# Feed forward of a two-layer hybrid block: 12 of 22 column pairs by seven block products instead of eight

## The chip, the cores and the metric

The kernel runs on one core of a Trainium2 chip. The metric is device time in microseconds (us). The engines are named as in the profile: PE is TensorE's matmul, PEld its weight load, DVE is VectorE, ACT is ScalarE, POOL is GpSimd, SP is SyncE, which here only issues DMAs.

## The reference, cut to what matters

Two layers run over a sequence of 528 positions (16 learned ones and 512 tokens). Each layer has four mixers, a merge of them, an output projection, and then the feed forward that is changed here:

```
D_MODEL, D_FF = 1024, 2816
x = x + merged @ w_out
h2 = rmsnorm(x, norm_ffn)
gt, up = jnp.split(h2 @ w_gu, 2, axis=-1)        # 1024 -> 2 x 2816
return x + (jax.nn.silu(gt) * up) @ w_down       # 2816 -> 1024
```

All numbers are 32-bit floats.

## The kernel before, in words

Activations are kept transposed: a tile has 128 features in its partitions and the positions in its columns. The normalised input `h2` is eight such tiles, `hh[0..7]`, with eight more, `hl[0..7]`, that hold what is left over, because every operand of TensorE is split into a high part (ACT casts it, `split`, L199, or `wload`, L190) and a low part (DVE subtracts, L200 or L192), and every product is made of three: high times high, high weight times low input, low weight times high input (`mmk`, L206).

The 2816 columns of the gate and of the up matrix are 22 blocks of 128. Pair j is block j of both: 1024 inputs to 128 gate columns and 128 up columns. Pair 0 is done by `head`, beside the end of the norm; the others by `mm`. A product of 1024 by 128 has eight k-steps of three matmuls. In layer 0 the 528 positions are two segments of 264 columns, so a pair has 2 x 8 x 3 x 2 = 96 matmuls of 264 columns; layer 1 needs 512 positions only, one segment, so a pair has 48 matmuls of 512 columns. Then ACT takes the tanh of the gate out of PSUM (L365), DVE makes silu(gate) times up (L366, L1584), and `split` makes `ah` and `al` of it, the operands of the down projection.

The pairs are done in three groups (8, 7 and 7 pairs, `FFG`); after each group the down projection adds that group's share to the residual (`residual`, L1545). Weights come in tiles of 128 by 512 (four k-steps): a DMA of SP into `wr` (3 buffers), the cast into `wh` and the subtraction into `wl` (5 buffers each).

PE's instructions stand in the order in which the program is written. The order of ACT, DVE, POOL and SP is set by a scheduler from the dependences, the buffers and its own estimates; `after(...)` holds what is issued inside it behind the instructions named. Generators (`start`, `pump`, `need`) lay side work between the matmuls. One of them is `s5_prep`, the tables of the state space mixer: those of layer 0 are made during the mixers of layer 0, those of layer 1 during the first pairs of the feed forward of layer 0.

PSUM is eight banks: `psm` gives two at a time (2 such buffers), `psx` one (4 buffers).

Of the kernel before, what the change touches and what calls it, by code (L numbers as in the profile page):

```python
# [9 lines left out]
F32 = mybir.dt.float32  # L10
F32R = mybir.dt.float32r
U32 = mybir.dt.uint32
AF = mybir.ActivationFunctionType
ALU = mybir.AluOpType
AX = mybir.AxisListType

P = 128
D = 1024
KD = D // P
SEQ = 512  # L20
META = 16
T = SEQ + META
DEPTH = 2
# [3 lines left out]
KF = FF // P  # L27
# [26 lines left out]
    _o += _w  # L54
NPK = _o
FFG = [(0, 8), (8, 7), (15, 7)]


def halves(segs):
    t0 = segs[0][0]  # L60
    n = (T - t0) // 2
    return [(t0, n), (t0 + n, n)]


class Kern:
# [36 lines left out]
    def after(self, *inss):  # L102

        ctx = ExitStack()
        for ins in inss:
            ctx.enter_context(self.tc.issue_after(ins))
        return ctx
# [1386 lines left out]
        return bh, bl  # L1494


    def layer(self, l, xdram, segs, after):
        nc, a = self.nc, self.a
        t0 = segs[0][0]
        st, gdn = self.gdn_proj(l)  # L1500
        self.share = False
        qk, rv = self.ret_proj(l)
        self.mg = []
        for j in range(KD):
            if j == 4:
                gs = self.head_gates(l, C_DG, segs)
                while "m" not in st["done"]:
                    self.pump()
            if j % 4 == 0:
                mg = self.f4(name="mg")  # L1510
            self.mg.append(mg[:, j % 4, :])
            self.gate(self.mg[j], l, 3, j, segs)
        parts = self.head_finish(gdn, st["v"], gs, self.par(l, "gdn"), segs)
        glap = self.gla_proj(l)
        gst, gla = next(glap)
        ret = self.start(self.ret_gen(l, qk, rv))
        pst = {"go": False}
        if l == 0:
            prep = self.start(self.s5_prep(0, pst))
        self.merge(l, 3, *parts, segs, "first")  # L1520
        next(glap)
        self.need(ret)
        gst["done"] += "v"
        pst["go"] = True
        self.merge(l, 1, *self.head_finish(ret, rv, self.head_gates(l, C_RG, segs), self.par(l, "rtn"), segs), segs, "mid")
        sy = self.s5_proj(l)
        if l == 0:
            self.need(prep)
        self.need(gla)
        zh, zl = self.f4(F32R, "zh"), self.f4(F32R, "zl")  # L1530
        s5 = self.s5_gens(l, sy, zh, zl, t0)
        self.merge(l, 0, *self.head_finish(gla, gst["v"], self.head_gates(l, C_HG, segs), self.par(l, "hgn"), segs), segs,
                   "mid")
        parts = self.s5_finish(l, s5, sy, zh, zl, segs)
        self.mh, self.ml = [], []
        self.merge(l, 2, *parts, segs, "last")
        xt = [self.f4(name="x") for _ in range(2)]
        xs = [xt[j // 4][:, j % 4, :] for j in range(KD)]
        self.norm_new(segs, xs, self.norm_h(self.par(l, "nffn")))

        def residual(srcs, kt, xh, xl, old, norm):

            tail = KD - 2 if norm else KD
            for j, ps in enumerate(self.mms(srcs[:tail], kt, xh, xl, segs)):
                nc.vector.scalar_tensor_tensor(out=self.sv(xs[j], segs), in0=ps, scalar=0.5,  # L1545
                                               in1=self.sv(old(j), segs), op0=ALU.mult, op1=ALU.add)
                if norm:
                    self.norm_sq(j, (t0, T - t0))
            if norm:
                olds = [old(j) for j in range(tail, KD)]  # L1550

                def evac(i, ps, h):
                    s0, n = halves(segs)[h]
                    c = slice(s0, s0 + n)
                    nc.vector.scalar_tensor_tensor(out=xs[tail + i][:, c], in0=ps, scalar=0.5, in1=olds[i][:, c],  # L1555
                                                   op0=ALU.mult, op1=ALU.add)
                    self.nrm["last"] = self.norm_sq(tail + i, (s0, n), own=l + 1 == DEPTH and kt < KD and i == h == 1)
                self.mm2h(srcs[tail:], kt, xh, xl, segs, self.tail_hooks(kt), evac)

        def xold(j):  # L1560
            xo = self.f(name="xo")
            nc.sync.dma_start(xo[:, t0:], xdram[j][:, t0:])
            return xo

        residual([a["w_out"][l, j] for j in range(KD)], KD, self.mh, self.ml, xold, True)

        prep = None
        for g0, gn in FFG:
            ah, al = [], []
            for j in range(gn):  # L1570
                if j % 4 == 0:
                    h4, l4 = self.f4(F32R, "ah"), self.f4(F32R, "al")
                srcs = [a["w_gu"][l, o + g0 + j] for o in (0, KF)]
                sg = segs
                if g0 + j == 0:
                    sg = halves(segs)
                    pg, pu = self.head(srcs, segs)
                else:
                    pg, pu = (self.mm(self.wload(s, KD), KD, self.hh, self.hl, segs) for s in srcs)
                if g0 + j == 2 and l + 1 < DEPTH:  # L1580
                    prep = self.start(self.s5_prep(l + 1, {"go": True}))
                s = self.f(name="s")
                self.silu2(s, pg, sg)
                nc.vector.tensor_tensor(out=self.sv(s, sg), in0=self.sv(s, sg), in1=pu, op=ALU.mult)  # L1584
                hv, lv = h4[:, j % 4, :], l4[:, j % 4, :]
                self.split(hv[:, t0:], lv[:, t0:], s[:, t0:])
                ah.append(hv)
                al.append(lv)
            last = g0 + gn == KF
            if last:  # L1590
                self.need(prep)
                self.norm_new(segs, xs, after(), then=KD if l + 1 < DEPTH else 0)
            residual([a["w_dn"][l, j, :, g0 * P:(g0 + gn) * P] for j in range(KD)], gn, ah, al, lambda j: xs[j], last)
        return xs
# [182 lines left out]
```

## Time and profile before

| | us |
|---|---|
| median of 3 runs | 2227.5 (2225.49 to 2228.37) |
| profiled execution | 2226.7 |
| its span | 2224.9 |
| PE busy | 2202.2 (99%) |
| DVE busy | 1269.9 (57%) |
| ACT busy | 893.7 (40%) |

The span is the time from the first to the last instruction in the trace; the profiled execution is 1.8 us longer and 0.8 us under the median. A matmul's own duration in the trace overlaps the next one's, so what a matmul costs is read from how many start in a stretch, not from its duration.

### The profile page before, as it was taken

How to read it: one execution, taken by the hardware profiler on the slowest of the kernel's cores; microseconds unless marked ns; L12 is line 12 of the kernel's file. 1: busy time of each engine (PE TensorE's matmuls, PEld its weight loads, DVE VectorE, ACT ScalarE, POOL GpSimd, SP SyncE). 2: the span in 40 equal slices, each digit the busy share in tenths (PEclk: the TensorE clock that was granted, in tenths of full speed). 3: DMA queues.
4: the chain of work that ended last, by engine and by line, in shares of the span. 5: the costliest groups of instructions: out<-in, count | busy, mean ns of one | idle time of the engine just before them, and what ended most of it. 6: DMA issues, size and time to landing. Idle time of an engine off the chain costs nothing. (4 is left out here: it accounts for less than half of the span.)

```text
span 2224.9 us, 41086 instructions
## 1 busy us (share of the span) xinstructions
PE 2202.2 (99%) x16300; PEld 2019.0 (91%) x16300; DVE 1269.9 (57%) x2505; ACT 893.7 (40%) x1920; POOL 189.5 (9%) x243
## 2 busy tenths in 40 slices
PE   9999999999999999999999999999999999999998
PEld 8999999999999999999999988787888888888887
DVE  7884566758444677533367844745385445434344
ACT  5653544433333433322346534644333334323232
POOL 2420021110000100000014121000000001000000
PEclk9999999999999999999999999999999999999999
DMA  4332222374233234332232332222643332332322
GB/s 129 104 105 66 86 77 77 111 228 141 89 91 119 96 110 124 124 87 94 88 119 83 106 95 83 75 72 72 202 122 90 95 123 91 90 100 91 98 93 83
DMA packets 144540, 229.73 MB, mean 103 GB/s; under 512 B 30044, under 2 KB 46884, under 8 KB 143836
## 3 DMA queue, kind: packets, MB, share of 16 engines
q1 hardware_dynamic: 136572, 208.98, 30.5%
q0 software_dynamic: 4032, 11.70, 1.6%
q10 hardware_dynamic: 3744, 6.42, 0.8%
q8 instruction: 128, 2.10, 0.4%
q14 instruction: 64, 0.52, 0.1%
HBM read 207.40 MB, written 19.65 MB: 102 GB/s over the span
## 5 line engine op out<-in xcount | busy, mean ns | idle before, releaser
L190 ACT CAST wh<-wr 128x512 fp32r<-128x512 f32 (+1 forms) x680 | 416.7, 614 | 1019.7 <-PE pm L206 841.7
L206 PE MATMUL pm<-hh,wh 128*128 128x264 f32 (+1 forms) x3120 | 799.6, 315 | 3.0 <-ACT hh L199 1.6
L206 PE MATMUL pm<-hl,wh 128*128 128x264 f32 (+1 forms) x3120 | 787.4, 312 | 5.6 <-POOL hl L200 2.9
L206 PE MATMUL pm<-hh,wl 128*128 128x264 f32 (+1 forms) x3120 | 783.2, 310 | 0.0
L192 DVE TENSOR_TENSOR wl<-wr,wh 128x512 fp32r<-128x512 f32 (+1 forms) x664 | 460.1, 695 | 537.3 <-ACT wh L190 528.3
L206 PEld LDWEIGHTS pm<-hh,wh 128*128 128x128 f32 x3120 | 513.5, 189 | 40.2 <-ACT hh L199 2.6
L206 PEld LDWEIGHTS pm<-hl,wh 128*128 128x128 f32 x3120 | 513.1, 189 | 38.9 <-POOL hl L200 4.4
L206 PEld LDWEIGHTS pm<-hh,wl 128*128 128x128 f32 x3120 | 512.8, 189 | 30.7
L206 PE MATMUL pm<-ah,wh 128*128 128x264 f32 (+2 forms) x542 | 146.0, 318 | 0.0
L206 PE MATMUL pm<-al,wh 128*128 128x264 f32 (+2 forms) x542 | 145.6, 317 | 0.0
L206 PE MATMUL pm<-ah,wl 128*128 128x264 f32 (+2 forms) x542 | 145.5, 317 | 0.0
L206 PE MATMUL pm<-bh,wh 128*128 128x264 f32 (+1 forms) x384 | 105.4, 328 | 0.8 <-DVE mg L445 0.5
L206 PE MATMUL pm<-bh,wl 128*128 128x264 f32 (+1 forms) x384 | 102.4, 321 | 0.0
L206 PE MATMUL pm<-bl,wh 128*128 128x264 f32 (+1 forms) x384 | 102.2, 320 | 0.0
L270 POOL TENSOR_TENSOR rs<-rs,mhalf 88x3 f32<-88x3 f32 (+1 forms) x10 | 8.4, 841 | 1060.1 <-ACT rs L269 1055.1
L206 PEld LDWEIGHTS pm<-ah,wh 128*128 128x128 f32 x542 | 91.4, 188 | 7.7 <-ACT wh L190 0.4
L206 PEld LDWEIGHTS pm<-al,wh 128*128 128x128 f32 x542 | 91.1, 188 | 7.2
L206 PEld LDWEIGHTS pm<-ah,wl 128*128 128x128 f32 x542 | 91.2, 188 | 6.9
L802 DVE SCALAR_TENSOR_TENSOR acc<-cvr,pk,acc 128x528 f32<-128x528 f32 x72 | 69.0, 960 | 8.8 <-ACT acc L799 7.9
L206 PEld LDWEIGHTS pm<-bh,wh 128*128 128x128 f32 x384 | 63.5, 188 | 8.1 <-DVE mg L445 1.3
L206 PEld LDWEIGHTS pm<-bh,wl 128*128 128x128 f32 x384 | 63.7, 188 | 5.4
L445 DVE SCALAR_TENSOR_TENSOR th<-th,pm 128x528 f32<-128x528 f32 (+1 forms) x48 | 33.3, 694 | 61.6 <-PE pm L206 55.4
(409 smaller groups left out, 2484.6 us busy)
## 6 DMA issues: line engine op xcount, KB each, us to landing
wr<-in_w_in SPq DMA_DIRECT2D x304, 256.0 KB, 2.7
wr<-in_w_gu SPq DMA_DIRECT2D x176, 256.0 KB, 2.6
wr<-in_w_br SPq DMA_DIRECT2D x64, 256.0 KB, 2.6
wr<-in_w_dn SPq DMA_DIRECT2D x64, 256.0 KB, 2.6
wr<-in_w_out SPq DMA_DIRECT2D x32, 256.0 KB, 2.6
wr<-in_w_dn SPq DMA_DIRECT2D x32, 192.0 KB, 2.4
s5mi<-s5m ACTq DMA_DIRECT2D x16, 256.0 KB, 3.1
mi<-s5mi SPq DMA_DIRECT2D x16, 256.0 KB, 3.7
```

Source lines behind the costliest of these rows:

```text
L190: i = nc.scalar.copy(hi[:, :n], raw[:, :n])
L192: j = eng.tensor_tensor(out=lo[:, :n], in0=raw[:, :n], in1=hi[:, :n].bitcast(F32), op=ALU.subtract)
L206: self.nc.tensor.matmul(ps[:m, i, :n], wt, x[k][:, t0:t0 + n], start=(k == 0 and i2 == 0), stop=(k == kt - 1 and i2 == 2))
L270: nc.gpsimd.tensor_tensor(out=dst, in0=dst, in1=self.mhalf[:dst.shape[0], :n], op=ALU.pow)
L445: nc.vector.scalar_tensor_tensor(out=self.sv(th, segs), in0=self.sv(th, segs), scalar=1.0, in1=br, op0=ALU.add, op1=ALU.mult)
L802: nc.vector.scalar_tensor_tensor(out=acc, in0=raw[:, w:w + T], scalar=conv[:, jt + w:jt + w + 1], in1=acc, op0=ALU.mult, op1=ALU.add)
```

## The change

A pair is a product of a 2 x 2 block matrix (gate and up, each with its first and second half of the 1024 inputs) with a 2 x 2 block matrix (first and second half of the inputs, first and second half of the positions). Done block by block that is eight products of 512 inputs by 128 columns by half the positions; the change does 12 of the 22 pairs of each layer (4, 5, 7, 8, 10, 11, 13, 14, 16, 17, 19, 20, `SEVEN`) by seven, in the form of Strassen's method with few sums. Both layers then use halves: 7 x 4 x 3 = 84 matmuls of 264 columns in layer 0 and 84 of 256 columns in layer 1.

Four sums of weight blocks (s1 to s4) are made on DVE for each such pair, and the seven left operands g0, s1, s2, g1, s3, s4, u1 are then split as weights are. Four sums of input blocks (T1 to T4) are made once a layer (`right_sums`), beside pairs 1 to 3, and kept. The products go to two banks, a and c, of one `psm` buffer and to one `psx` bank, d. Bank a takes four of the products one upon the other (g0, s2, s3, u1) and bank c two (s1, s4); between them ACT copies the sum so far into SBUF (`keep`), and DVE adds up the rest (`add`).

Pairs that keep eight products (`pair8`) have the matmuls of before. All pairs but the first are written as units: a unit of a `pair7` is one product (12 matmuls), a unit of a `pair8` four k-steps of one matrix. `units` writes the operands of unit i+4 ahead of the products of unit i, and holds them behind the last three copies or sums that read PSUM.

`s5_prep` of layer 1 moves from the feed forward of layer 0 to the mixers of layer 1, to the place that it has in layer 0.

```diff
+SEVEN = [j for j in range(4, KF) if j % 3]
+    def right_sums(self, segs):
...
+        for k in range(4):
+            top, low = self.f(name="xk"), self.f(name="xk")
+            for dst, kk in ((top, k), (low, k + 4)):
+                nc.vector.tensor_tensor(out=dst[:, t0:], in0=self.hh[kk][:, t0:].bitcast(F32),
+                                        in1=self.hl[kk][:, t0:].bitcast(F32), op=ALU.add)
...
+                if i == 0:
+                    nc.vector.tensor_tensor(out=x, in0=b12, in1=b11, op=ALU.subtract)
+                    nc.vector.tensor_tensor(out=y, in0=b22, in1=x, op=ALU.subtract)
+                    nc.vector.tensor_tensor(out=b21, in0=b21, in1=y, op=ALU.subtract)
+                    sums = (1, 2)
+                else:
+                    nc.vector.tensor_tensor(out=x, in0=b22, in1=b12, op=ALU.subtract)
+                    nc.scalar.copy(y, b21)
+                    sums = (3, 4)
...
+                self.split(hi[:, :2 * n], lo[:, :2 * n], t[:, :2 * n])
...
+    def pair7(self, srcs, segs, finish):
...
+        def load():
+            for key, src, c in (("g0", 0, 0), ("u0", 1, 0), ("u1", 1, 512), ("g1", 0, 512)):
+                v[key] = self.ch("raw").rearrange("p a b -> p (a b)")
+                nc.sync.dma_start(v[key], srcs[src][:, c:c + 512])
+        def comb(key, x, y, op):
+            v[key] = self.ch("sum").rearrange("p a b -> p (a b)")
+            nc.vector.tensor_tensor(out=v[key], in0=v[x], in1=v[y], op=op)
+        def operands(key):
+            def run():
...
+                elif key == "s1":
+                    comb("s1", "u0", "u1", ALU.add)
+                elif key == "s2":
+                    comb("s2", "s1", "g0", ALU.subtract)
+                elif key == "s3":
+                    comb("s3", "g0", "u0", ALU.subtract)
+                elif key == "s4":
+                    comb("s4", "g1", "s2", ALU.subtract)
+                hi = self.wp.tile([P, 512], F32R, tag="wh", name="wh", bufs=5)
+                lo = self.wp.tile([P, 512], F32R, tag="wl", name="wl", bufs=5)
+                self.split(hi, lo, v[key])
...
+        def products(key, to, x, first):
...
+                for k in range(4):
+                    ks = slice(k * P, k * P + P)
+                    xh, xl = x(k)
+                    for i, (wt, xx) in enumerate(((hi, xh), (hi, xl), (lo, xh))):
+                        nc.tensor.matmul(v[to], wt[:, ks], xx, start=(first and k == 0 and i == 0),
+                                         stop=(k == 3 and i == 2), skip_group_check=True)
+        def keep(dst, src):
+            return lambda: [nc.scalar.copy(v[dst], v[src]).ins]
+        def add(dst, src):
+            return lambda: [nc.vector.tensor_tensor(out=v[dst], in0=v[src], in1=v[dst], op=ALU.add).ins]
+        def rest():
+            return add(("G", 1), "c")() + add(("U", 1), ("U", 0))()
+        return [(operands("g0"), products("g0", "a", B(0, 0), True), keep(("G", 0), "a")),
+                (operands("s1"), products("s1", "c", T(1), True), keep(("U", 1), "c")),
+                (operands("s2"), products("s2", "a", T(2), False), keep(("G", 1), "a")),
+                (operands("g1"), products("g1", "d", B(1, 0), True), add(("G", 0), "d")),
+                (operands("s3"), products("s3", "a", T(3), False), keep(("U", 0), "a")),
+                (operands("s4"), products("s4", "c", B(1, 1), False), rest),
+                (operands("u1"), products("u1", "a", T(4), False), last)]
...
+    def units(self, us, ahead=4):
+        made, pins = 0, []
+        for i, (_, products, then) in enumerate(us):
+            while made < min(i + ahead + 1, len(us)):
+                with self.after(*pins):
+                    us[made][0]()
+                made += 1
+            products()
+            pins = (pins + then())[-3:]
 def layer(self, l, xdram, segs, after):
...
-        if l == 0:
-            prep = self.start(self.s5_prep(0, pst))
+        prep = self.start(self.s5_prep(l, pst))
...
-                    pg, pu = (self.mm(self.wload(s, KD), KD, self.hh, self.hl, segs) for s in srcs)
-                if g0 + j == 2 and l + 1 < DEPTH:
-                    prep = self.start(self.s5_prep(l + 1, {"go": True}))
...
+                    us += (self.pair7 if g0 + j in SEVEN else self.pair8)(srcs, segs, finish)
+                if g0 + j == 3:
+                    self.units(us)
+                    us = []
+                    self.need(sums)
+            self.units(us)
```

After a pair by seven the `finish` function takes the tanh of the gate from SBUF (L1745), multiplies by the gate (L1746), and by up in two halves (L1749), one of which is still in bank a.

The first place at which the order matters is ACT's queue in the feed forward of layer 0, in the last group of pairs; of before:

```order
L190 CAST wh<-wr 128x512 x2
L365 ACTIVATE th<-pm 128x528
L190 CAST wh<-wr 128x512 x2
L199 CAST ah<-s 128x528
L190 CAST wh<-wr 128x512 x2
L365 ACTIVATE th<-pm 128x528
L190 CAST wh<-wr 128x512 x2
L199 CAST ah<-s 128x528
```

Four weight casts, one tanh and one cast of the result stand for each pair, and none of them is waited for by the next matmul but through the weights.

The same queue in the changed kernel, from the middle of pair 10 to the third copy of pair 11, two pairs by seven that follow each other (`raw` and `sum` are the left operands, `COPY G` and `COPY U` what `keep` takes out of banks a and c):

```order
L200 CAST wh<-sum 128x512
L1600 COPY U<-pm 128x264
L200 CAST wh<-sum 128x512
L200 CAST wh<-raw 128x512
L1745 ACTIVATE s<-G 128x528
L200 CAST wh<-sum 128x512
L1600 COPY G<-pm 128x264
L200 CAST ah<-s 128x528
L200 CAST wh<-sum 128x512
L1600 COPY U<-pm 128x264
L200 CAST wh<-raw 128x512
L1600 COPY G<-pm 128x264
```

The copies of pair 11 now stand behind pair 10's tanh and behind the cast of its result, which waits for DVE.

DVE's queue of before, in the same group:

```order
L366 SCALAR_TENSOR_TENSOR s<-th,pm 128x528
L192 TENSOR_TENSOR wl<-wr,wh 128x512
L1584 TENSOR_TENSOR s<-s,pm 128x528
L192 TENSOR_TENSOR wl<-wr,wh 128x512
L200 TENSOR_TENSOR al<-s,ah 128x528
L192 TENSOR_TENSOR wl<-wr,wh 128x512 x2
```

That is one pair: four subtractions for the weights and three instructions for the result.

DVE's queue of the changed kernel, between the same two pairs 10 and 11 (`sum<-` are the sums of weight blocks, `G<-px` and `G<-pm` the sums that read PSUM):

```order
L1603 TENSOR_TENSOR U<-U 128x264
L201 TENSOR_TENSOR wl<-sum,wh 128x512
L1603 TENSOR_TENSOR G<-pm,G 128x264
L1552 TENSOR_TENSOR sum<-raw 128x512
L201 TENSOR_TENSOR wl<-raw,wh 128x512
L1746 SCALAR_TENSOR_TENSOR s<-s,G 128x528
L1552 TENSOR_TENSOR sum<-raw,sum 128x512
L1749 TENSOR_TENSOR s<-s,U 128x264
L1749 TENSOR_TENSOR s<-s,pm 128x264
L201 TENSOR_TENSOR wl<-sum,wh 128x512
L201 TENSOR_TENSOR al<-s,ah 128x528
L201 TENSOR_TENSOR wl<-sum,wh 128x512
```

Pair 10's result (L1746, L1749) now stands among the sums and subtractions for pair 11's operands.

## Rows read from the trace of the kernel before

**Rows 1.** The page, parts 1 and 2: busy us and instructions; granted clock in tenths.
```profile
PE 2202.2 (99%) x16300; PEld 2019.0 (91%) x16300; DVE 1269.9 (57%) x2505; ACT 893.7 (40%) x1920; POOL 189.5 (9%) x243
PEclk9999999999999999999999999999999999999999
```
**Rows 2.** Stretches, feed forward of layer 0: us, then PE, PEld, DVE, ACT, POOL busy (count), clock, DMA.
```profile
757.00:930.00 173.00, 173.00 (x1459) 171.63 (x1458) 115.90 (x261) 61.91 (x112) 10.91 (x17) 1.00 0.38 122
```
**Rows 3.** Stretches, line L206 alone, layer 0 and layer 1: PE busy (count), PEld busy (count), clock, DMA.
```profile
1000.00:1055.00 55.00, 55.00 (x453) 55.00 (x452) 1.00 0.29 95
1950.00:2000.00 50.00, 50.00 (x217) 40.56 (x216) 1.00 0.31 95
```
**Rows 4.** Timeline, PE, end of layer 1: start us, us; 37 matmuls of 256 columns.
```profile
2203.73 0.28 PE L206 MATMUL pm<-al,wh 128*128 128x256 f32 x1
...
2207.99 0.28 PE L206 MATMUL pm<-al,wh 128*128 128x256 f32 x1
```
**Rows 5.** Groups by form, DVE, us 870 to 1010: count, busy us, mean ns, idle before.
```profile
L192 DVE TENSOR_TENSOR wl<-wr,wh 128x512 fp32r<-128x512 f32 x40 | 27.6, 689 | 40.5 <-ACT wh L190 40.4
L200 DVE TENSOR_TENSOR al<-s,ah 128x528 fp32r<-128x528 f32 x7 | 5.0, 707 | 0.6
L1584 DVE TENSOR_TENSOR s<-s,pm 128x528 f32<-128x528 f32 x7 | 4.9, 703 | 11.1 <-PE pm L206 11.1
L366 DVE SCALAR_TENSOR_TENSOR s<-th,pm 128x528 f32<-128x528 f32 x7 | 4.9, 698 | 0.0
L1171 DVE TENSOR_TENSOR s5u<-s5pw,s5m 128x512 f32<-128x512 f32 x8 | 5.1, 685 | 0.0
```
**Rows 6.** Groups by form, DVE, whole span, and line L1555 (ns min/median/max): half-width instructions.
```profile
L295 DVE TENSOR_TENSOR acc<-acc,sq 128x264 f32<-128x264 f32 x20 | 8.6, 431 | 2.7 <-ACT sq L291 2.5
...
L1555 DVE SCALAR_TENSOR_TENSOR x<-pm,x x8: 424/426/435, 1135.0 to 2214.2; 128x264 f32<-128x264 f32 x4, 128x256 f32<-128x256 f32 x4
```
**Rows 7.** Groups by form, ACT, us 870 to 1010; the last row from the whole span.
```profile
L190 ACT CAST wh<-wr 128x512 fp32r<-128x512 f32 x40 | 24.9, 621 | 75.0 <-PE pm L206 71.4 <-issue 3.6
L199 ACT CAST ah<-s 128x528 fp32r<-128x528 f32 x7 | 4.4, 635 | 2.4 <-DVE s L1584 2.4
L365 ACT ACTIVATE th<-pm 128x528 f32<-128x528 f32 x7 | 4.2, 606 | 0.0
...
L1360 ACT COPY u<-pm 128x264 f32<-128x264 f32 x16 | 5.3, 382 | 0.0
```
**Rows 8.** Chain that ended last, in order: start us, us, what.
```profile
2208.07 0.43 DVE x L1555
...
2208.59 0.43 ACT sq L291
2209.01 0.02 issue
```
**Rows 9.** DMA issues of the page: KB each, us to landing.
```profile
wr<-in_w_gu SPq DMA_DIRECT2D x176, 256.0 KB, 2.6
```
**Rows 10.** Stretches, all engines: mixers of layer 0 with its tables, then mixers of layer 1.
```profile
222.00:560.00 338.00, 338.00 (x3209) 326.40 (x3209) 232.04 (x560) 148.39 (x360) 37.68 (x54) 1.00 0.39 120
...
1229.00:1614.00 385.00, 381.91 (x2787) 327.25 (x2786) 213.04 (x449) 174.74 (x410) 39.04 (x42) 1.00 0.33 100
```
**Rows 11.** Stretches, all engines: around the two norms ahead of the feed forward, and one in layer 1.
```profile
741.00:745.00 4.00, 2.67 (x21) 2.15 (x19) 4.00 (x9) 1.44 (x5) 1.19 (x2) 1.00 0.37 120
745.00:748.00 3.00, 2.21 (x9) 1.91 (x10) 2.75 (x4) 1.16 (x4) 1.87 (x3) 0.50 0.05 20
748.00:752.00 4.00, 4.00 (x21) 4.00 (x21) 2.18 (x6) 1.23 (x4) 0.34 (x1) 0.53 0.02 4
1842.00:1846.00 4.00, 2.40 (x14) 2.11 (x12) 3.33 (x7) 1.87 (x6) 2.43 (x3) 0.76 0.22 66
1846.00:1850.00 4.00, 4.00 (x30) 4.00 (x30) 2.21 (x6) 1.37 (x4) 0.81 (x1) 0.82 0.00 0
...
1242.00:1248.00 6.00, 4.51 (x26) 3.60 (x25) 4.32 (x14) 5.05 (x20) 0.00 (x0) 1.00 0.07 26
```
**Rows 12.** Waits of PE, us 1224 to 1279: us in total, times, longest.
```profile
PE px L974 <- DVE gam L976: 1.5, 1, 1.5
```

More of the change, by code (lines that the diff above doesn't have):

```diff
@@ L1494, in s5_finish @@
         return bh, bl
+    def right_sums(self, segs):
+        nc = self.nc
+        (a0, n), (b0, _) = halves(segs)
+        t0 = a0
+        self.T = {}
+        rows = [self.f4(F32R, "xsum") for _ in range(2)]
+        for k in range(4):
[3 more added lines that the diff above has]
+                                        in1=self.hl[kk][:, t0:].bitcast(F32), op=ALU.add)
+            b11, b12, b21, b22 = (x[:, c:c + n] for x in (top, low) for c in (a0, b0))
+            yield
+            for i in range(2):
+                t = self.f(name="xt")
+                x, y = t[:, 0:n], t[:, n:2 * n]
+                if i == 0:
[7 more added lines that the diff above has]
+                    sums = (3, 4)
+                if i == 0:
+                    hi, lo = self.b(name="xsh"), self.b(name="xsl")
+                else:
+                    hi, lo = (r[:, k, :] for r in rows)
+                self.split(hi[:, :2 * n], lo[:, :2 * n], t[:, :2 * n])
+                for j, c in zip(sums, (0, n)):
+                    self.T[j, k] = (hi[:, c:c + n], lo[:, c:c + n])
+                yield
@@ new lines, in pair7, with B, T, run @@
+    def pair7(self, srcs, segs, finish):
+        nc = self.nc
+        hs = halves(segs)
+        n = hs[0][1]
+        v = {}
+        def load():
[7 more added lines that the diff above has]
+            def run():
+                if key == "g0":
+                    load()
+                elif key == "s1":
[9 more added lines that the diff above has]
+                self.split(hi, lo, v[key])
+                v[key, 0], v[key, 1] = hi, lo
+            return run
+        def B(i, j):
+            s0 = hs[j][0]
+            return lambda k: (self.hh[4 * i + k][:, s0:s0 + n], self.hl[4 * i + k][:, s0:s0 + n])
+        def T(j):
+            return lambda k: self.T[j, k]
+        def products(key, to, x, first):
+            def run():
+                if key == "g0":
+                    pa = self.psm()
+                    v["a"], v["c"] = pa[:, 0, :n], pa[:, 1, :n]
+                    for name in ("G", "U"):
+                        t = self.f(name=name)
+                        v[name, 0], v[name, 1] = (t[:, s0:s0 + n] for s0, _ in hs)
+                        v[name] = t
+                if to == "d":
+                    v["d"] = self.psx([P, 512])[:, :n]
+                hi, lo = v[key, 0], v[key, 1]
+                for k in range(4):
[4 more added lines that the diff above has]
+                                         stop=(k == 3 and i == 2), skip_group_check=True)
+            return run
+        def keep(dst, src):
[4 more added lines that the diff above has]
+            return add(("G", 1), "c")() + add(("U", 1), ("U", 0))()
+        def last():
+            finish(v["G"], (v["a"], v["U", 1]))
+            return []
+        return [(operands("g0"), products("g0", "a", B(0, 0), True), keep(("G", 0), "a")),
[5 more added lines that the diff above has]
+                (operands("u1"), products("u1", "a", T(4), False), last)]
@@ new lines, in pair8, with operands, run, products @@
+    def pair8(self, srcs, segs, finish):
+        nc = self.nc
+        v = {}
+        def operands(i, h):
+            def run():
+                raw = self.wp.tile([P, 512], F32, tag="wr", name="wr", bufs=3)
+                hi = self.wp.tile([P, 512], F32R, tag="wh", name="wh", bufs=5)
+                lo = self.wp.tile([P, 512], F32R, tag="wl", name="wl", bufs=5)
+                nc.sync.dma_start(raw, srcs[i][:, 512 * h:512 * h + 512])
+                self.split(hi, lo, raw)
+                v[i, h] = lambda k: tuple(t[:, (k % 4) * P:(k % 4) * P + P] for t in (hi, lo))
+            return run
+        def products(i, h):
+            def run():
+                self.pump()
+                if h == 0:
+                    v[i] = self.psm()
+                for k in range(4 * h, 4 * h + 4):
+                    self.mmk(v[i], v[i, h], k, KD, self.hh, self.hl, segs)
+            return run
+        def last():
+            finish(self.pv(v[0], segs), self.pv(v[1], segs))
+            return []
+        return [(operands(i, h), products(i, h), last if i and h else lambda: []) for i in range(2) for h in range(2)]
@@ L1526, in layer @@
         sy = self.s5_proj(l)
-        if l == 0:
-            self.need(prep)
+        self.need(prep)
         self.need(gla)
@@ L1565, in layer, with finish @@
         residual([a["w_out"][l, j] for j in range(KD)], KD, self.mh, self.ml, xold, True)
-        prep = None
         for g0, gn in FFG:
-            ah, al = [], []
+            ah, al, act = [], [], [None, None]
+            us = []
             for j in range(gn):
-                if j % 4 == 0:
-                    h4, l4 = self.f4(F32R, "ah"), self.f4(F32R, "al")
                 srcs = [a["w_gu"][l, o + g0 + j] for o in (0, KF)]
-                sg = segs
+                def finish(pg, pu, j=j, sg=segs):
+                    if j % 4 == 0:
+                        act[:] = self.f4(F32R, "ah"), self.f4(F32R, "al")
+                    s = self.f(name="s")
+                    if len(pg.shape) == 3:
+                        self.silu2(s, pg, sg)
+                        nc.vector.tensor_tensor(out=self.sv(s, sg), in0=self.sv(s, sg), in1=pu, op=ALU.mult)
+                    else:
+                        nc.scalar.activation(s[:, t0:], pg[:, t0:], AF.Tanh, scale=0.5)
+                        nc.vector.scalar_tensor_tensor(out=s[:, t0:], in0=s[:, t0:], scalar=1.0, in1=pg[:, t0:],
+                                                       op0=ALU.add, op1=ALU.mult)
+                        for (s0, n), u in reversed(list(zip(halves(segs), pu))):
+                            nc.vector.tensor_tensor(out=s[:, s0:s0 + n], in0=s[:, s0:s0 + n], in1=u, op=ALU.mult)
+                    hv, lv = (t[:, j % 4, :] for t in act)
+                    self.split(hv[:, t0:], lv[:, t0:], s[:, t0:])
+                    ah.append(hv)
+                    al.append(lv)
@@ L1575, in layer @@
                 if g0 + j == 0:
-                    sg = halves(segs)
-                    pg, pu = self.head(srcs, segs)
-                else:
-                    pg, pu = (self.mm(self.wload(s, KD), KD, self.hh, self.hl, segs) for s in srcs)
-                if g0 + j == 2 and l + 1 < DEPTH:
-                    prep = self.start(self.s5_prep(l + 1, {"go": True}))
-                s = self.f(name="s")
-                self.silu2(s, pg, sg)
-                nc.vector.tensor_tensor(out=self.sv(s, sg), in0=self.sv(s, sg), in1=pu, op=ALU.mult)
@@ L1585, in layer @@
[L1585 to L1588, printed above, removed]
+                    finish(*self.head(srcs, segs), sg=halves(segs))
+                    sums = self.start(self.right_sums(segs))
+                else:
+                    us += (self.pair7 if g0 + j in SEVEN else self.pair8)(srcs, segs, finish)
+                if g0 + j == 3:
+                    self.units(us)
+                    us = []
+                    self.need(sums)
@@ L1589, in layer @@
+            self.units(us)
             last = g0 + gn == KF
             if last:
-                self.need(prep)
                 self.norm_new(segs, xs, after(), then=KD if l + 1 < DEPTH else 0)
```

## The prediction

> **What bounds the kernel now.** I read the page first. PE is busy 99% of the span, DVE 57%, ACT 40%, and the granted clock is full in all slices at this resolution [rows 1]. A busy PE alone proves nothing, so I went to a stretch of the feed forward: from 757 to 930 us PE is never idle while DVE is busy two thirds of the time [rows 2]. The reader is to see there that in these stages only a matmul taken away, or a wait put in, moves the end. Then I took what one matmul costs from counts, since its own duration overlaps the next one's. In layer 0, 453 matmuls of 264 columns fill 55.00 us: 0.1214 us each. In layer 1, 217 of 512 columns fill 50.00 us: 0.2304 us each [rows 3]. Of 256 columns the run has little, but in the last down projection 36 intervals take 2207.99 - 2203.73 = 4.26 us: 0.1183 us each [rows 4]. So two matmuls of 256 columns cost 0.006 us more than one of 512, and the weight load that each one needs stays hidden at that pace.
>
> **What goes from PE.** Layer 0: 12 pairs x (96 - 84) matmuls x 0.1214 = 17.5 us. Layer 1: a pair of eight is 48 x 0.2304 = 11.06 us, a pair of seven 84 x 0.1183 = 9.94 us, and 12 x 1.12 = 13.5 us. Together 31.0 us, all of it on the path. The PE work of the tables (`s5_prep`) is only moved.
>
> **What is added on DVE and ACT.** A pair of seven has on DVE seven subtractions of 0.689 us, four sums of weight blocks for which I take the 0.685 us of another sum of two 128x512 tiles from SBUF, and for the result 0.698 and 0.707 us [rows 5], and five half-width instructions of about 0.43 us [rows 6]: 4.82 + 2.74 + 1.41 + 2.14 = 11.1 us. A pair of eight has 4 x 0.689 + 0.703 + 0.698 + 0.707 = 4.9 us. ACT has 7 x 0.621 + 4 x 0.382 + 0.606 + 0.635 = 7.1 us in a pair of seven (0.382 is a copy of 264 columns out of PSUM), 3.7 us in a pair of eight [rows 7]. PE needs 84 x 0.1214 = 10.2 us for a pair of seven and 11.7 us for one of eight in layer 0. So DVE is slower than PE in a pair of seven by about 1 us and far faster over the pattern seven, seven, eight (27.1 us of DVE against 32.1 us of PE). The average is covered; the question is the order within two pairs of seven that follow each other.
>
> **The wait that comes instead.** Bank a takes g0, s2, s3 and u1 one upon the other, with one product between; before each next one ACT must have copied the bank out. A product lasts 12 x 0.1214 = 1.457 us, and its sum can be read about 0.2 us after the next has begun (a matmul lasts 0.28 us and starts every 0.12 [rows 4]). That leaves 1.26 us for a copy of 0.38 us and two hand-overs. From DVE to ACT a hand-over takes 0.09 us (2208.07 + 0.43 to 2208.59), the next one starts 0.02 us after ACT's end at the earliest [rows 8]; I take 0.05 us. The copy is in time as long as ACT gets to it within 0.8 us.
>
> I walked pairs 10 and 11 through the queues, with zero at pair 10's start, where DVE is still idle at times. Up to DVE's sums for pair 11 nothing is late: the copies end at 2.1, 3.6 and 5.0 us, due at 2.9, 7.3 and 5.8; that of s3 ends at 8.6, due at 8.7. From 8.25 us on DVE has no gap: subtraction for s1, sum of U, subtraction for s2, sum of G, sum s3, subtraction for g1, the silu product, sum s4 and two half products, 5.85 us, to 14.1. Only then can ACT cast pair 10's result, and behind that cast stand in ACT's queue the cast of s4, the copy of U, the cast of u1 and the third copy: 14.15 + 0.635 + 0.62 + 0.38 + 0.62 + 0.38 = 16.8 us. Pair 11's s3 is due at 11 x 1.457 = 16.0. PE waits 0.8 us. Its later copies follow the delayed products and are in time again, and the pair of eight that follows, with 2.9 us for a unit, lets DVE catch up.
>
> This happens where two pairs of seven adjoin in one group: 4-5, 10-11, 13-14, 16-17, 19-20. (7 and 8 are parted by a down projection.) At 13-14 the scheduler puts a weight cast of the down projection ahead of the third copy, which adds 0.62 us. Layer 0: 4 x 0.8 + 1.4 = 4.6 us. In layer 1 a product lasts 1.42 us, s3 is due at 15.6, the chain on DVE and ACT moves up by about 0.3 us only: 4 x 0.9 + 1.5 = 5.1 us. Together 9.7 us, with 0 (all copies in time) and 22 us (1.2 us more at each of the ten, were each of the 25 steps of that chain 0.05 us longer) as the ends.
>
> Where a pair of seven follows one of eight there is no such wait: the tanh of the eight can run when its first matrix is done, 5.8 us before its end, so only one product, 0.7 us, and one cast, 0.635 us, precede the copy of g0, which ends at about 2 us and is due at 2.9.
>
> **The sums of the inputs.** Per layer 8 full sums, 16 half ones and 8 subtractions, 5.6 + 6.9 + 5.7 = 18.2 us of DVE, fall into pairs 1 to 3, beside 3 x 4.9 us of their own: 32.9 of 35.0 us in layer 0, about 32 of 33.2 in layer 1. The weights of these pairs are made four units ahead, 11 us, so PE does not run dry; what may be late is the first pair of seven. I take 0.5 us a layer, between 0 and 2.
>
> **The moved tables.** In the mixers of layer 0 they are made with DVE busy 232 of 338 us and no idle PE; those of layer 1 have DVE busy 213 of 385 us now [rows 10]. I take 0, between -1 and 5 us. Should the cover fail, PE waits for the state space mixer of layer 1.
>
> **DMA.** The same bytes come, four tiles at a time for a pair of seven, in SP's one queue, behind which the next weights stand. A tile lands 2.6 us after its issue [rows 9], and the scheduler issues those of a pair of seven a pair or more ahead; nothing is added.
>
> The sum, against the profiled execution: 2226.7 - 31.0 + 9.7 + 1.0 = 2206.4. That execution lies 0.8 us under the median, so 2207 is what I expect of a median.
>
> **Rivals.** First, no wait: the copies all keep their time, for which speaks that the margin is missed by 0.8 us after a chain of 16 us. The time is then 2227.5 - 31.0 = 2196.5. Against it speaks that DVE's total in a pair of seven exceeds PE's, whatever the order.
>
> Second, the lag is deeper: the 22 us of above instead of 9.7. 2219. For it speak the many changes between engines in that stretch and the copy of U that is in time by only 0.1 us; against it that DVE's instructions follow each other without gaps in the rows of the same kind.
>
> Third, the clock, which makes it slower. Around the norm ahead of the feed forward PE is idle for 1.33 us of the 4 us from 741, and the granted clock is 0.50 to 0.53 (1.2 of 2.4 GHz) from 745 to 752: (1 - 0.50) x 3 + (1 - 0.53) x 4 = 3.4 us lost. In layer 1 it is idle for 1.6 us of 4, and 0.24 x 4 + 0.18 x 4 = 1.7 us are lost [rows 11]. If each of the ten waits brought that down upon it, 17 to 34 us would go on top of 2207: 2224 to 2241, 2232 in the middle, slower than before. It decides from about 1.6 us lost at each. Against it: from 1242 to 1248 PE waits once for 1.5 us [rows 12] and the granted clock stays 1.00 [rows 11]; the waits of my walk are no longer and lie 20 to 30 us apart. The Trainium skill ("TensorE: Matmul & The Clock Gate", on the second HAM failure mode, psum-queue depth-cycling) says that short idles between groups of matmuls that cycle through PSUM banks can make the clock go back and forth. By that rule this rival would be the likely one; of the two places here, the trace agrees at the norms and not at 1242 us.
>
> **How the numbers follow.** The forecast has 0.71, no wait 0.10, the deeper lag 0.12, the clock 0.05, other mishaps that end slower 0.02. The time is the forecast's, 2207. The range goes from 2196, the case without waits, to 2220, just above the deeper lag; the clock's case and the worst of the others lie outside. About 0.2%, 4.5 us, is what a measurement of this kernel tells from no change, so under 2223 counts as faster. Forecast, first rival and nearly all of the second are: 0.90. Within 0.2% lie a part of the second and the mildest clock case: 0.04. Slower: 0.06.
>
> **What would show it.** Right: matmuls in all 16300 - 12 x 12 + 12 x 36 = 16588; in the feed forward PE idle at the third copy (L1600) of pairs 5, 11, 14, 17 and 20 in both layers, 0.8 to 1.5 us each, and hardly elsewhere; DVE busy up by about 24 x 6.2 + 36 = 185 us; the clock falling only at the norms; PE's idle time in the mixers of layer 1 as before. Wrong: waits for weights (L201) or for the input sums, waits in every pair of seven, a pace of the 256-column matmuls other than 0.118 us, half clock in the feed forward, or PE waiting in the state space mixer of layer 1.

## The result, and the profile after

The changed kernel takes 2276.07 us (2274.78 to 2278.5, 4 runs), the kernel before 2227.93: a ratio of 1.0217, with 1.0205 to 1.0230 as its 95% interval. It is 2.2% slower, 48 us, where 2207 us was forecast. The profiled execution's span is 2274.5 us, 49.6 more than before.

The first lines of the page after answer to [rows 1]:

```profile
span 2274.5 us, 42130 instructions
...
PE 2198.3 (97%) x16588; PEld 2019.8 (89%) x16588; DVE 1423.9 (63%) x2833; ACT 972.3 (43%) x2110; POOL 190.0 (8%) x243
...
PEclk9999999999999999999999999999999999999999
```

The count of matmuls is the forecast one, 16588, and PE's busy time fell. What grew is the time in which PE is not busy: 2274.5 - 2198.3 = 76 us, against 23 before. The waits of PE over the whole span (us in total, times, longest) say where:

```profile
PE pm L1595 <- ACT U L1600: 27.1, 48, 0.9
PE pm L1595 <- DVE G L1603: 12.5, 24, 0.5
PE pm L1595 <- ACT G L1600: 11.2, 24, 0.5
PE pm L207 <- POOL hl L201: 3.0, 4, 1.0
```

L1595 is a matmul of a pair by seven. The waits are 96, four in each of the 24 pairs, all on reads of PSUM, 50.8 us; the fourth row is the norm's, as before. The second of two adjoining pairs does not stand out: in layer 0 PE is idle 0.47, 0.47, 0.76 and 0.53 us in pair 4 and 0.47, 0.47, 0.47 and 0.53 us in pair 5. Which products wait is seen in the timeline of PE at the start of pair 4 in layer 0 (start us, us, in brackets the idle time and what ended it); the product with `hh` is g0, into bank a, the first with `xsh` is s1, into bank c, the second is s2, into bank a again:

```profile
799.85 0.28 PE L1595 MATMUL pm<-hh,wl 128*128 128x264 f32 x1
800.60 0.39 PE L1595 MATMUL pm<-xsh,wh 128*128 128x264 f32 x1 [0.47 <-ACT G L1600]
800.83 0.29 PE L1595 MATMUL pm<-xsl,wh 128*128 128x264 f32 x1
...
802.04 0.28 PE L1595 MATMUL pm<-xsh,wl 128*128 128x264 f32 x1
802.79 0.39 PE L1595 MATMUL pm<-xsh,wh 128*128 128x264 f32 x1 [0.47 <-ACT U L1600]
```

and ACT beside it:

```profile
800.17 0.38 ACT L1600 COPY G<-pm 128x264 f32<-128x264 f32 x1
800.44 0.62 ACT L200 CAST wh<-sum 128x512 fp32r<-128x512 f32 x1
802.36 0.38 ACT L1600 COPY U<-pm 128x264 f32<-128x264 f32 x1 [1.29 <-PE pm L1595]
```

s1 opens a bank of its own, c, and yet starts 0.05 us after the copy of bank a has ended. s2 writes bank a, whose copy is long done, and starts after the copy of bank c. So PE stands still for each copy that it was meant to run beside: s1 was due at 799.97 and starts 0.63 us late, and its second matmul another 0.11 us later than the pace. ACT is not behind in these two: before the second copy it sat idle for 1.29 us, waiting for PE.

One wait of the four has ACT's queue in it as well. In pair 4 the cast of s4's operand, which waited for DVE, stands ahead of the copy of s3's sum:

```profile
807.14 0.28 PE L1595 MATMUL pm<-xsum,wl 128*128 128x264 f32 x1
807.23 0.62 ACT L200 CAST wh<-sum 128x512 fp32r<-128x512 f32 x1 [1.77 <-DVE sum L1552]
807.76 0.37 ACT L1600 COPY U<-pm 128x264 f32<-128x264 f32 x1
808.18 0.39 PE L1595 MATMUL pm<-hh,wh 128*128 128x264 f32 x1 [0.76 <-ACT U L1600]
```

The copy starts 0.34 us after s3's last matmul has ended, instead of 0.04. This share is small: the 24 copies of U after s1 cost PE as much as the 24 of G, 11.2 us, so the 24 after s3 cost 27.1 - 11.2 = 15.9 us, some 4.7 us more than the same waits without a queue.

The granted clock is not part of it. Stretches with the waits in layer 0 and layer 1 (PE, PEld, DVE, ACT, POOL busy, clock, DMA):

```profile
800.00:820.00 20.00, 16.84 (x128) 15.65 (x127) 13.25 (x24) 9.81 (x21) 0.00 (x0) 1.00 0.04 14
920.00:980.00 60.00, 52.68 (x405) 49.72 (x404) 40.10 (x69) 26.29 (x51) 0.00 (x0) 1.00 0.19 61
1905.00:1965.00 60.00, 53.57 (x337) 46.89 (x335) 39.80 (x69) 27.46 (x54) 0.00 (x0) 1.00 0.27 86
```

By stage, the feed forward of layer 1 is the cleanest to compare, since no tables are made in it in either kernel. It runs from the last residual of the output projection to the last of the down projection. The line that adds them is L1555 before and L1718 after (ns min/median/max, first and last start us). Before, it began after

```profile
L1555 DVE SCALAR_TENSOR_TENSOR x<-pm,xo x8: 409/425/433, 730.6 to 1840.2; 128x264 f32<-128x264 f32 x4, 128x256 f32<-128x256 f32 x4
```

and ended at 2214.2 [rows 6]: 374.0 us. After:

```profile
L1718 DVE SCALAR_TENSOR_TENSOR x<-pm,xo x8: 411/425/433, 733.3 to 1865.9; 128x264 f32<-128x264 f32 x4, 128x256 f32<-128x256 f32 x4
L1718 DVE SCALAR_TENSOR_TENSOR x<-pm,x x8: 424/426/433, 1150.8 to 2263.8; 128x264 f32<-128x264 f32 x4, 128x256 f32<-128x256 f32 x4
```

2263.8 - 1865.9 = 397.9 us, 23.9 more. With 13.5 us of matmuls gone, something of 37.4 us has come in 12 pairs, 3.1 us in each.

### The profile page after: what moved, and what is told of

Read it like the earlier page. It is cut to its first block, busy times and chain, and to the rows that moved or that the text cites. A ratio compares the mean times of both kernels' runs of the same rounds, so it can differ in the third digit from the quotient of the medians.

```text
span 2274.5 us, 42130 instructions
## 1 busy us (share of the span) xinstructions
PE 2198.3 (97%) x16588; PEld 2019.8 (89%) x16588; DVE 1423.9 (63%) x2833; ACT 972.3 (43%) x2110; POOL 190.0 (8%) x243
## 4 chain that ended last, share of the span: by engine, by line
PE 87%; DVE 5%; ACT 4%; issue 2%; DMA 1%; POOL 1%; SPq 0%; DVEq 0%; ACTq 0%; POOLq 0%
PE pm L207 67%; PE pm L1595 10%; DVE acc L803 1%; PE px L1595 1%; PE px L471 1%; ACT U L1600 1%; DVE G L1603 1%; PE px L1451 1%; PE px L1454 1%; ACT wh L200 1%; DMA blkg<-dg 1%; PE px L400 1%; DVE wl L193 1%; ACT G L1600 0%; PE px L477 0%
## 5 line engine op out<-in xcount | busy, mean ns | idle before, releaser
L207 PE MATMUL pm<-hh,wh 128*128 128x264 f32 (+1 forms) x2544 | 647.0, 315 | 2.2 <-ACT hh L200 1.7
L207 PE MATMUL pm<-hl,wh 128*128 128x264 f32 (+1 forms) x2544 | 633.5, 309 | 5.6 <-POOL hl L201 3.0
L207 PE MATMUL pm<-hh,wl 128*128 128x264 f32 (+1 forms) x2544 | 630.0, 308 | 0.0
L191 ACT CAST wh<-wr 128x512 fp32r<-128x512 f32 (+1 forms) x512 | 312.3, 612 | 704.1 <-PE pm L207 561.8
L193 DVE TENSOR_TENSOR wl<-wr,wh 128x512 fp32r<-128x512 f32 x496 | 340.2, 688 | 339.8 <-ACT wh L191 325.0
L207 PEld LDWEIGHTS pm<-hh,wh 128*128 128x128 f32 x2544 | 418.5, 189 | 30.5 <-ACT hh L200 2.9
L207 PEld LDWEIGHTS pm<-hl,wh 128*128 128x128 f32 x2544 | 418.4, 189 | 29.4 <-POOL hl L201 4.2
L207 PEld LDWEIGHTS pm<-hh,wl 128*128 128x128 f32 x2544 | 417.9, 189 | 22.6
L201 DVE TENSOR_TENSOR wl<-raw,wh 128x512 fp32r<-128x512 f32 x72 | 49.6, 689 | 63.8 <-ACT wh L200 63.8
L201 DVE TENSOR_TENSOR wl<-sum,wh 128x512 fp32r<-128x512 f32 x96 | 66.0, 687 | 36.9 <-ACT wh L200 36.4
L1595 PE MATMUL pm<-xsum,wh 128*128 128x264 f32 (+1 forms) x384 | 73.7, 289 | 12.5 <-DVE G L1603 12.5
```

What stands on the lines that cost most here:

```text
L191: i = nc.scalar.copy(hi[:, :n], raw[:, :n])
L193: j = eng.tensor_tensor(out=lo[:, :n], in0=raw[:, :n], in1=hi[:, :n].bitcast(F32), op=ALU.subtract)
L201: (eng or nc.vector).tensor_tensor(out=lo, in0=src, in1=hi.bitcast(F32), op=ALU.subtract))
L207: self.nc.tensor.matmul(ps[:m, i, :n], wt, x[k][:, t0:t0 + n], start=(k == 0 and i2 == 0), stop=(k == kt - 1 and i2 == 2))
L1595: nc.tensor.matmul(v[to], wt[:, ks], xx, start=(first and k == 0 and i == 0), stop=(k == 3 and i == 2), skip_group_check=True)
```

## Experiments

**A tile for each bank.** In the code, banks a and c are the two halves of one tile: `pa = self.psm()`, `v["a"], v["c"] = pa[:, 0, :n], pa[:, 1, :n]`. Theory A: the library that turns tiles into waits keeps one record for the tile, so a product into one half waits for the reads of the other half. Theory B: ACT's queue is late, as in the forecast, only everywhere. Theory C: the loss is in the moved tables or in the units. The edit gives bank c a tile of its own:

```diff
-                    v["a"], v["c"] = pa[:, 0, :n], pa[:, 1, :n]
+                    v["a"], v["c"] = pa[:, 0, :n], self.psx([P, 512])[:, :n]
```

> Edit: bank c of a pair of seven becomes a one-bank tile of its own (psx) instead of the second half of the two-bank tile (psm) that holds bank a. Theory A (one tile for two banks): in the changed kernel s1, s2, s4 and u1 each wait for the read of the other bank's last sum, 4 waits in each of 24 pairs, 0.63 to 0.92 us from the due start and 0.11 more for the restart, about 3.3 us a pair, 79 us in all. With a tile for each bank these go, and what is left is the lag between two adjoining pairs of seven: 2276 - 79 + 10 = 2207 us, between 2197 and 2220, PE idle in the feed forward under 12 us. Theory B (ACT's queue is late at each product, whatever the tiles): the copies are as late as before, s2, s3 and u1 still wait, the time stays within 2255 to 2280 us. Theory C (the loss is not in the pairs of seven but in the moved tables or the units): 2270 to 2280 us.

Measured: 2199.86 us (2198.05 to 2200.78), ratio 0.9876 (0.9861 to 0.9890). The time falls by 76.2 us against the changed kernel, 0.79 us for each of the 96 waits. In the feed forward of layer 1, us 1820 to 2190, PE's waits are the norm's alone:

```profile
PE pm L207 <- POOL hl L201: 1.5, 2, 1.0
PE pm L207 <- ACT hh L200: 0.8, 2, 0.6
PE px L309 <- ACT sq L292: 0.7, 1, 0.7
PE pm L207 <- DVE hl L201: 0.4, 1, 0.4
```

and s1 (now `px`) follows g0, and s2 follows s1, at the pace of 0.12 us:

```profile
798.28 0.28 PE L1595 MATMUL pm<-hh,wl 128*128 128x264 f32 x1
798.40 0.28 PE L1595 MATMUL px<-xsh,wh 128*128 128x264 f32 x1
...
799.74 0.28 PE L1595 MATMUL px<-xsh,wl 128*128 128x264 f32 x1
799.86 0.28 PE L1595 MATMUL pm<-xsh,wh 128*128 128x264 f32 x1
```

The time lies in theory A's range, 7 us under its middle, and B and C fall. A copy of one bank and a product into the other do run beside each other on the chip; only the wait kept them apart. What the library keeps inside is not shown; that it orders these instructions by the tile is, since the wait goes when bank c has a tile of its own. One thing was not expected: the lag of 10 us between adjoining pairs that A still carried did not come either.

**The moved tables alone**, in the kernel before:

```diff
-        if l == 0:
-            prep = self.start(self.s5_prep(0, pst))
+        prep = self.start(self.s5_prep(l, pst))
...
-                if g0 + j == 2 and l + 1 < DEPTH:
-                    prep = self.start(self.s5_prep(l + 1, {"go": True}))
```

> The kernel before with one part of the change alone: the tables of layer 1 made during the mixers of layer 1. Theory A and B: within 5 us of the kernel before (2223 to 2233 us), since DVE has room there; of the 9.9 us by which the stretch between the two feed forwards grew, all but 1 to 3 us is PE's own work on the tables, which leaves the feed forward of layer 0. Theory C: 2245 us or more.

Measured: 2229.17 us (10 runs), ratio 1.0012 (1.0001 to 1.0022), so 0.2 to 4.9 us. The prediction's bounds of -1 and 5 held; its 0 lies just outside the interval.

**No pair by seven**, all else as in the changed kernel:

```diff
-SEVEN = [j for j in range(4, KF) if j % 3]
+SEVEN = []
```

> The changed kernel with no pair by seven: units, input sums (made but not used) and moved tables stay. Theory A and B: 2226 to 2234 us, no waits in the feed forward, since 24 pairs by eight bring back the matmuls of before. Theory C: 2260 us or more. Against the changed kernel this gives what 24 pairs by seven cost as they are: about 2276 - 2229 = 47 us, 2.0 us a pair, which must be 3.3 us of waits less 1.3 us of matmuls.

Measured: 2230.79 us (10 runs), ratio 1.0014 (1.0004 to 1.0023). The units, the input sums and the moved tables together cost 0.9 to 5.1 us. The changed kernel's 24 pairs by seven thus cost 2276.07 - 2230.79 = 45.3 us, and with a tile for each bank they give 2230.79 - 2199.86 = 30.9 us, where 31.0 was worked out from the pace of the matmuls. That they agree to 0.1 us is luck: the intervals of the two ratios allow some 4 us either way.

**One layer only.** If the shared tile is the whole cause, its cost is by the wait. Here layer 0 keeps the shared tile:

```diff
-                    v["a"], v["c"] = pa[:, 0, :n], self.psx([P, 512])[:, :n]
+                    v["a"], v["c"] = pa[:, 0, :n], (self.psx([P, 512])[:, :n] if hs[0][0] else pa[:, 1, :n])
```

> Edit: banks a and c in one tile in layer 0, as in the changed kernel, and in tiles of their own in layer 1, as in e1_own_banks. Theory A (each of the four products waits for the read of the other bank because both are one tile; 76.2 us for 96 waits, 0.79 each): 48 waits remain, 2199.9 + 38 = 2238 us, between 2233 and 2243, all in layer 0. If the waits of one layer came from something else that the tile only sets off (the clock, the order of ACT as a whole), it would not be half: 2215 or less, or 2255 or more.

Measured: 2239.45 us (2236.73 to 2242.93), ratio 1.0061 (1.0046 to 1.0076): 39.6 us over a tile for each bank, 0.82 for each of 48 waits (41 us and 0.86 by the ratios, since the two versions were timed against different runs of the kernel before). PE's waits, whole span:

```profile
PE pm L1595 <- ACT U L1600: 13.5, 24, 0.9
PE pm L1595 <- DVE G L1603: 6.3, 12, 0.5
PE pm L1595 <- ACT G L1600: 5.6, 12, 0.5
```

They are half as many and half as long in total, and all of them lie in layer 0.

**All pairs from 4 on by seven.** The lag that did not come asks whether DVE really needs 11.1 us for a pair by seven. If it does, longer runs of such pairs must run dry:

```diff
-SEVEN = [j for j in range(4, KF) if j % 3]
+SEVEN = list(range(4, KF))
```

(with a tile for each bank)

> Edit: a tile for each bank, as in e1_own_banks, and all pairs from 4 to 21 by seven, 18 a layer instead of 12. It asks why the lag between adjoining pairs of seven (9.7 us in the prediction) did not come. Theory D (on DVE and ACT one instruction starts before the one before it has ended: 0.60 us between starts where each lasts 0.68, 0.34 where each lasts 0.42, so a pair of seven needs about 7 x 0.61 + 4 x 0.60 + 5 x 0.34 + 2 x 0.62 = 9.6 us of DVE, less than PE's 10.2 and 9.9): runs of 4 and 7 pairs of seven keep up, and 6 more pairs a layer give 6 x (1.457 + 1.12) = 15.5 us: 2184 us, between 2180 and 2190. Theory E (a pair of seven needs the 11.1 us of the durations, and in e1 the pairs of eight between them caught up): each further pair in a run is 0.9 to 1.2 us late, 18 pairs a layer less what four units of lead absorb, 3 to 4 us a run: 2195 to 2210 us, with waits for L201 or L1600 at the end of each run.

Measured: 2181.14 us (2179.5 to 2181.89), ratio 0.9799 (0.9783 to 0.9816). This is the fastest version, 2.0% under the kernel before. Six more pairs a layer take the ratio from 0.9876 to 0.9799, some 17 us by the ratios, where 15.5 were worked out. Between us 888 and 950, in a run of seven such pairs, PE is never idle, and DVE is at 94%:

```profile
888.00:950.00 62.00, 62.00 (x513) 62.00 (x513) 58.52 (x107) 39.85 (x79) 0.00 (x0) 1.00 0.28 90
```

Theory D's number came and E's did not, and no matmul of a pair by seven waits in the whole span. DVE, as busy as that, still keeps PE's pace. The durations of its 107 instructions in this stretch add up to 65.3 us, more than the 62 us in which they ran, and busy time, which counts what overlaps once, is 58.5 us: this is the run that says that the durations overstate what DVE needs.

## Why the prediction was wrong

**The step that failed** is the one that priced the wait: "before each next one ACT must have copied the bank out", and "with one product between". I put the wait on the bank, so that each copy had a whole product to hide behind. The waits are on the tile, and a and c are one tile. So s1 waits for the copy of g0's sum, s2 for that of s1, s4 for that of s3, u1 for DVE's reading of bank c: four products of seven have nothing between, and g0, g1 and s3 alone find the other reads long done. The prediction named waits in every pair of seven as a sign of being wrong, and they came. Nothing in the trace of before had to be known for this. The line with `pa[:, 0, :n], pa[:, 1, :n]` stands in the change, and each wait is in the built program, at the first matmul of s1, s2, s4 and u1; with a tile for each bank, in pair 4, that of s1 waits for the cast of its weights and that of s2 for the copy of bank a. I walked the queues of ACT and DVE and not what PE itself waits for.

What a wait costs can be followed in rows, all at hand before but the last: 0.28 us for the last matmul to end instead of 0.12, a hand-over, 0.38 us for the copy, another hand-over, and one slow start of 0.11 us, seen in the trace after. That is 0.74 us in the timeline above. Over all 96 waits it is the 50.8 us of idle time and 96 x (0.16 + 0.11) = 25.9 us of late ends and slow starts, an estimate of 76.7 us; the experiment has 76.2, or 0.79 for each.

**The matmuls taken away**: forecast 31.0 us, measured 30.9. The pace of 0.1183 us for 256 columns [rows 4], from 36 intervals at the end of the run, held.

**The lag between two adjoining pairs of seven**, forecast 9.7 us: measured none, with a tile for each bank. The mechanism was thought through with durations where starts are what counts. DVE in pair 4 and 5 of that run, from the subtraction for g1 to the second half product:

```profile
806.75 0.68 DVE L201 TENSOR_TENSOR wl<-raw,wh 128x512 fp32r<-128x512 f32 x1
807.35 0.68 DVE L1552 TENSOR_TENSOR sum<-raw 128x512 f32<-128x512 f32 x1
807.95 0.70 DVE L1746 SCALAR_TENSOR_TENSOR s<-s,G 128x528 f32<-128x528 f32 x1
808.57 0.68 DVE L1552 TENSOR_TENSOR sum<-raw,sum 128x512 f32<-128x512 f32 x1
809.17 0.42 DVE L1749 TENSOR_TENSOR s<-s,U 128x264 f32<-128x264 f32 x1
809.51 0.42 DVE L1749 TENSOR_TENSOR s<-s,pm 128x264 f32<-128x264 f32 x1
```

One of 0.68 us starts 0.60 us after the one before, one of 0.42 us leaves 0.34. On ACT the same: a copy of 0.38 us and the next cast 0.27 us later:

```profile
810.51 0.37 ACT L1600 COPY U<-px 128x264 f32<-128x264 f32 x1
810.78 0.62 ACT L200 CAST wh<-raw 128x512 fp32r<-128x512 f32 x1
811.72 0.38 ACT L1600 COPY G<-pm 128x264 f32<-128x264 f32 x1 [0.32 <-PE pm L1595]
```

Pair 4 starts at 796.9 there. The chain that I put at 5.85 us, from the subtraction for s1 at 804.85 to the end of the second half product at 809.93, took 5.1 us. The third copy, forecast to end at 16.8 us and due at 16.0, ended at 812.10, 15.2 us after pair 4's start, and ACT had to wait for PE before it. The scheduler had also moved one cast ahead of the cast of the result in this version; by the starts above the old order would have been in time as well (13.07, where the cast of the result starts, + 0.54 + 0.60 + 0.27 + 0.60 + 0.38 = 15.5), but that order was not run without the shared tile. The trace of before shows the overlap too, had I looked; two instructions of DVE that follow each other there:

```profile
888.47 0.68 DVE L192 TENSOR_TENSOR wl<-wr,wh 128x512 fp32r<-128x512 f32 x1
889.07 0.68 DVE L1171 TENSOR_TENSOR s5t<-s5pw,rot 128x512 f32<-128x512 f32 x1
```

The sentence of the prediction that DVE's total in a pair of seven exceeds PE's fails with it: by starts it is about 9.6 us against 10.2. DVE's busy time in the changed kernel rose by 1423.9 - 1269.9 = 154.0 us, where 185 was forecast from durations. The Trainium skill names an overlap of this kind ("Perfetto Trace Analysis", section "Optimizing Scalar/DVE Operations": part of an instruction's profiled latency overlaps with the next one); the rows agree, with 0.08 us for DVE and 0.11 us for ACT.

**The input sums and the tables**, forecast 1.0 and 0 us: 0.9 to 5.1 us together. Small, and inside the bounds.

**The clock**, the rival that ended slower: it named the right side for a wrong reason. 96 waits of about half a microsecond, up to four in 12 us, left the granted clock at 1.00 in all the stretches above. The Trainium skill's rule on short idles between groups of matmuls, cited in the prediction ("TensorE: Matmul & The Clock Gate", the second HAM failure mode), did not come about at these waits.

The sum with the waits put in: 2227.9 - 31.0 (by the pace of the matmuls) + 2.3 (units, sums and tables, by medians) + 76.7 (the waits, by the trace after) = 2275.9, against 2276.1. With the experiments' 30.9 and 76.2 in place of 31.0 and 76.7 it would show nothing, since both are taken from the same medians and the sum closes by itself.

## What to carry to other kernels

When the gain of a change rests on a copy running beside the next product, look at what the next product's first matmul waits for, tile by tile: banks that are filled and emptied in turn want tiles of their own, or the library orders them one after the other. Price a busy engine by the distance between starts of instructions that follow each other, as PE is priced, and not by durations. And a kernel that is slower by 2% can hold a gain of 2%: it took one line here to go from 2276 to 2200 us, and one more to 2181.

## What the runs showed of the hardware that was not expected

ACT and DVE read one PSUM bank while PE writes another at full pace: with a tile for each bank no matmul of a pair by seven waited, and the pace was 0.1214 us a matmul from 796.95 to 817.23 us (layer 0) and 0.1182 from 1909.58 to 1919.39 us (layer 1), beside the 96 copies of ACT. Repeated short stops of PE (16% of the time between 800 and 820 us) did not lower its granted clock. At the norms ahead of the feed forward it does fall: PE is idle 1.33 us of the 4 us from 741 and 0.79 us of the next 3, in which the clock is 0.50; in layer 1 it is idle 1.60 us of 4, at 0.76 [rows 11]. The idle time of one such stretch does not tell the two apart: in the changed kernel PE is idle 1.29 us of the 4 us from 806.5, nearly the 1.33 of the norm, and the clock stays at 1.00; PE does not stop in the 3 us behind them. What makes the difference stays open.
